# Plain down blocks and the u3 sums reach the residual by accumulating transfers, in a two-layer GLA and stick-breaking decoder trunk

## The chip, the core and the metric

The kernel runs on one core of a Trainium2 chip. The metric is the device time of one execution, in microseconds. The core's engines work side by side: TensorE multiplies matrices (PE in the profile), VectorE (DVE), ScalarE (ACT), GpSimd (POOL) and SyncE (SP), whose work here is to issue transfers. Sixteen DMA engines carry the transfers of all queues. Each engine runs its own instructions in order and waits on semaphores for what other engines or transfers have to deliver.

## The reference, cut to what is computed

One input `x` of 512 tokens by 1024 features in float32 passes two layers. Each is an FFN with half a step, a mixer, and a second FFN with half a step; a final RMSNorm ends it.

```python
def swiglu(h, w_gate, w_up, w_down):
    return (jax.nn.silu(h @ w_gate) * (h @ w_up)) @ w_down

for i in range(DEPTH):                       # DEPTH = 2
    x = x + 0.5 * swiglu(rmsnorm(x, ffn1_norm[i]), ffn1_w_gate[i], ffn1_w_up[i], ffn1_w_down[i])
    h = rmsnorm(x, mix_norm[i])
    y = gla_mixer(...) if i % N_MIXERS == 0 else sb_mixer(...)
    x = x + y
    x = x + 0.5 * swiglu(rmsnorm(x, ffn2_norm[i]), ffn2_w_gate[i], ffn2_w_up[i], ffn2_w_down[i])
return rmsnorm(x, final_norm)
```

So there are four FFNs: the first, the second after the gated linear attention, the third, and the last after the stick-breaking attention. The hidden width of an FFN is 2816, that is 11 chunks of 256 columns.

## The kernel before, in words

**The residual.** It stays on the core, transposed: eight tiles `xs[0]` to `xs[7]` of 128 features by 512 tokens in float32. Every down product of an FFN adds half of its result to one of these tiles.

**Products in parts.** TensorE multiplies each float32 product as three: every weight and every activation is split into a high and a low part, and high x high, low x high and high x low are added in one PSUM bank (`mm3`, line 80). The split of a weight is a cast on ScalarE (`wh`, L138) and a subtraction on VectorE (`wl`, L139). Weights arrive in blocks of 1 MB for gate and up (tile `raw`, two buffers) and 512 KB for down (`rawd`), issued on SyncE's queue at L105.

**The FFN.** `FFN.GROUPS` cuts the 11 chunks into six groups: chunks 0-1, 2-3, 4-5, 6-7, 8 and 9-10. A group's gate and up products give hidden tiles; its down products follow while the next group's gate and up run. Three kinds of product occur.

- *Seven products* for gate and up (`seven`): a Strassen-like scheme computes a 2x2 block product in seven instead of eight. VectorE first forms sums of weight blocks, `sums_12` and `sums_34` (L704, L705, L710, L711), from the raw block into a tile `s`; these sums are then split like weights. In PSUM the banks `ps_w`, `ps_q` and `ps_z` are built up over several products. ScalarE copies `ps_w` into `ps_z` (L746), so that TensorE can go on in both; later it copies an intermediate sum into the tile `u3` (L764), and VectorE adds it (L765).
- *Seven downs* (`seven_down`) for groups 1 and 3, in the same scheme. Their result is added to the residual a quarter at a time by `add` on VectorE (L396). One intermediate sum, `u3`, belongs to two quarters: ScalarE copies it from PSUM (L435), VectorE adds the copy to the right half of a tile of the upper residual half, and the bank is used on for other quarters.
- *Plain downs* (`down`) for groups 0, 2, 4 and 5. Each call is a part: `n` parts in a group of `n` hidden blocks, with `8 / n` residual tiles in each. For the tiles that `homes` names, ScalarE writes half of the PSUM bank into a tile `d` (L340), and a transfer that accumulates, on GpSimd's queue, adds it to the residual tile (L341, 256 KB). For the others VectorE adds half of the bank to the residual itself (L345).

`HOMES` (L624) lists per group which tiles go by transfer, by the tag of the place that holds `d`: `("d",)` for groups 0 and 2, `("d", "ss", "sq")` for group 4; the places are single. `ss` and `sq` also hold the sums of squares and the factor `R` of the norm, and the t34 parts of the seven downs. The gate and up sevens' `u3` is tagged `c` in the pool `tp`, with one buffer, and the seven downs' `u3` shares it.

**The order of the work.** Each engine's order is set by a planner of the framework, which places the instructions by its own costs; TensorE's order follows a queue of entries (`feed.q`), one per weight block, and many pieces are pinned behind the last matmul. A place is written again only when its last reader, a transfer too, is done.

**The end.** In the last FFN the down products of the last group are computed with tokens on partitions (`back_tok`). Before them `to_tokens` transposes the eight residual tiles on TensorE into `ps_T` (L1570), and ScalarE copies them back (L1575); the final norm follows on the tokens.

The list of groups and the part of the code that hands the homes on:

```python
GROUPS = ((0, 2), (2, 4), (4, 6), (6, 8), (8, 9), (9, 11))
DOWN_SEVEN = (1, 3)
HOMES = {0: ("d",), 2: ("d",), 4: ("d", "ss", "sq")}
...
homes = self.HOMES.get(group, ())
downs = [
    (wd, c0 * 256, n, self.hs[group], part, nxt if end else None, 0, homes) for part in range(n)
]
```

Of the kernel before, what the change touches and what calls it, by code (L numbers as in the profile page):

```python
# [10 lines left out]
F32 = mybir.dt.float32  # L11
# [3 lines left out]
AF = mybir.ActivationFunctionType  # L15
ALU = mybir.AluOpType
PSUM = bass.MemoryType.PSUM

P = 128
T = 512  # L20
# [10 lines left out]
def turns(t):  # L31

    return t.rearrange("p (two n) -> p n two", two=2)


def flat(ps):

    return ps.rearrange("p (n two) -> p two n", two=2)


def pair(t):

    return t.rearrange("p (two n) -> p two n", two=2)
# [3 lines left out]
def decoder(ctx: ExitStack, tc: tile.TileContext, a: dict, out: bass.AP):  # L47
    nc = tc.nc
# [6 lines left out]
    sp = ctx.enter_context(tc.tile_pool(name="sp", bufs=1))  # L55
# [5 lines left out]
    def psum(name, tag=None):  # L61
        if tag is None:
            tag = order[turn_[0] % 8]
            turn_[0] += 1
        return pp.tile([P, T], F32, tag=tag, bufs=banks[tag], name=name)
# [11 lines left out]
    xs = [xp.tile([P, T], F32, name=f"x{k}") for k in range(KD)]  # L77
# [4 lines left out]
    def mm3(ps, wh, wl, mh, ml, first, last):  # L82
        mm(ps, wh, turns(mh), first, False)
        mm(ps, wl, turns(mh), False, False)
        mm(ps, wh, turns(ml), False, last)
# [223 lines left out]

                feed.q.append(Entry([u], body))  # L310

    def down(w, r0, nf, hs, part, nxt, late=0, homes=()):


        nd = KD // nf
        src = w[r0 : r0 + nf * P, part * nd * P : (part + 1) * nd * P]
        ch = Chunk(src.rearrange("(f p) c -> p f c", p=P), nf, nd * P)
        ch.few = True

        def body(W):  # L320
            (wh, wl), = W
            acc = []

            def prod(m, fs):
                if m == len(acc):
                    acc.append(psum("ps_d"))
                s = slice(m * P, (m + 1) * P)
                for f in fs:
                    mm3(acc[m], wh[:, f, s], wl[:, f, s], hs[f][0], hs[f][1], f == 0, f == nf - 1)

            if late:
                for m in range(nd):
                    prod(m, range(nf - late))
            for m in range(nd):
                prod(m, range(nf - late if late else 0, nf))
                ps = acc[m]
                k = part * nd + m
                if m < len(homes):
                    d = sp.tile([P, T], F32, tag=homes[m], name="d")
                    nc.scalar.activation(pair(d), flat(ps), AF.Copy, scale=0.5)  # L340
                    nc.gpsimd.dma_start(xs[k], d, accum_op=ALU.add)  # L341
                    yield
                    continue
                x = pair(xs[k])
                nc.vector.scalar_tensor_tensor(  # L345
                    out=x, in0=flat(ps), scalar=0.5, in1=x, op0=ALU.mult, op1=ALU.add
                )
                if nxt is not None:
                    nxt(k)
                yield  # L350

        feed.q.append(Entry([(ch, lambda t: t, nf, nd * P)], body))

    def seven_down(pool, w, r0, hs, part):

        H = T // 2
        lower, upper = (
            Chunk(w[r0 : r0 + 4 * P, c : c + 256].rearrange("(f p) c -> p f c", p=P), 4, 256)  # L360
            for c in (part * 256, 512 + part * 256)
        )
        lower.few = upper.few = True
        v = {}

        def halves():

            lo, up = (c.load().rearrange("p (c two) d -> p two c d", two=2) for c in (lower, upper))
            return lo[:, 0], lo[:, 1], up[:, 0], up[:, 1]

        def sums_12(_):
            a11, _, a21, a22 = halves()
            s = v["s12"] = pool().tile([P, 4, 256], F32, tag="s", bufs=4, name="s12")
            nc.vector.tensor_tensor(out=s[:, 0:2], in0=a21, in1=a22, op=ALU.add)
            nc.vector.tensor_tensor(out=s[:, 2:4], in0=s[:, 0:2], in1=a11, op=ALU.subtract)
            return s

        def sums_34(_):
            a11, a12, a21, _ = halves()
            s = pool().tile([P, 4, 256], F32, tag="s", bufs=4, name="s34")  # L380
            nc.vector.tensor_tensor(out=s[:, 0:2], in0=a11, in1=a21, op=ALU.subtract)
            nc.vector.tensor_tensor(out=s[:, 2:4], in0=a12, in1=v["s12"][:, 2:4], op=ALU.subtract)
            return s

        def prod(ps, w, k0, m, b, first):
            for c in range(2):
                bh, bl = (turns(t) for t in hs[c][b])
                wh, wl = (t[:, k0 + c, m * P : (m + 1) * P] for t in w)
                for n, (l_, r_) in enumerate(((wh, bh), (wl, bh), (wh, bl))):
                    st["pe"] = nc.tensor.matmul(  # L390
                        ps, l_, r_, start=first and c + n == 0, stop=c == 1 and n == 2, skip_group_check=True
                    ).ins

        def add(m, up, col, ps):
            x = pair(xs[part * 2 + m + 4 * up][:, col * H : col * H + H])
            nc.vector.scalar_tensor_tensor(out=x, in0=ps, scalar=0.5, in1=x, op0=ALU.mult, op1=ALU.add)  # L396

        def body_1(W):
            a11, s, v["a2"] = W
            ws, zs, qs = [], [], []  # L400
            for m in range(2):
                ws.append(psum("ps_w")[:, 0:H])
                prod(ws[m], a11, 0, m, "b11", True)
            for m in range(2):


                zs.append(psum("ps_z")[:, 0:H])
                nc.scalar.copy(zs[m], ws[m])
            yield

            ps = psum("ps_q")
            for m in range(2):
                qs.append(ps[:, m * H : (m + 1) * H])
                prod(qs[m], s, 0, m, "t1", m == 0)
            for m in range(2):
                add(m, 1, 1, flat(qs[m]))
            yield
            for m in range(2):
                prod(ws[m], s, 2, m, "t2", False)
                add(m, 0, 1, flat(ws[m]))  # L420
            yield
            for m in range(2):
                prod(zs[m], v["a2"], 0, m, "b21", False)
                add(m, 0, 0, flat(zs[m]))
            v["w"], v["q"] = ws, qs
            yield

        def body_2(W):
            (s,) = W
            ws, qs = v["w"], v["q"]  # L430

            u3 = pool().tile([P, 2, H], F32, tag="c", bufs=1, name="u3")
            for m in range(2):
                prod(ws[m], s, 0, m, "t3", False)
                nc.scalar.copy(pair(u3[:, m]), flat(ws[m]))  # L435
                add(m, 1, 1, pair(u3[:, m]))
            yield
            for m in range(2):
                prod(qs[m], s, 2, m, "b22", False)
            for m in range(2):  # L440
                add(m, 0, 1, flat(qs[m]))
            yield
            for m in range(2):
                prod(ws[m], v["a2"], 2, m, "t4", False)
                add(m, 1, 0, flat(ws[m]))
            yield

        units = [(lower, lambda t: halves()[0], 2, 256), (lower, sums_12, 4, 256), (lower, lambda t: halves()[1::2], 4, 256)]
        feed.q.append(Entry(units, body_1))
        feed.q.append(Entry([(lower, sums_34, 4, 256)], body_2))  # L450

    def back_tok(w, r0, nf, hs, done):
# [160 lines left out]
    class FFN:  # L613
# [7 lines left out]
        NORMED, SEVEN, AHEAD = 6, 2, 2  # L621
        DOWN_SEVEN = (1, 3)
        SEVEN_UP = (2, 3, 4, 5, 6, 7, 8, 9, 10)
        HOMES = {0: ("d",), 2: ("d",), 4: ("d", "ss", "sq")}  # L624

        def __init__(self, wg, wu, wd, gi, nxt, first=False, last=False):
            self.gi, self.normed = gi, False
# [4 lines left out]
            base, downs, late = len(feed.q), [], []  # L632
            self.sums_by = 10**6
            for group, (c0, c1) in enumerate(self.GROUPS):
                slots, put = 2 * (c1 - c0), 0
                if group == 1:

                    for put in range(self.AHEAD):
                        down(*downs[put][:6], late=put == 0, homes=homes)
                    put = self.AHEAD  # L640
                for i in range(slots):
                    c, f = c0 + i // 2, i % 2
                    if f == 0:
                        g, u = Chunk(cols(wg, c * 256, 256), KD, 256), Chunk(cols(wu, c * 256, 256), KD, 256)
                    d = self.defer if i == 0 and c == 0 else None
# [30 lines left out]
                for x in downs[put:]:  # L676
                    down(*x)
                n = 2 * (c1 - c0)
                end = group + 1 == len(self.GROUPS)
                homes = self.HOMES.get(group, ())  # L680
                downs = [
                    (wd, c0 * 256, n, self.hs[group], part, nxt if end else None, 0, homes) for part in range(n)
                ]
                if group in self.DOWN_SEVEN:
                    downs = []
# [1228 lines left out]
```

## Time and profile before

| | |
|---|---|
| median of 3 runs | 1779.24 us (1779.19 to 1779.93) |
| profiled execution | 1779.44 us |
| its span in the trace | 1777.5 us |
| TensorE busy | 1756.3 us, 12714 instructions |
| VectorE busy | 1508.6 us, 2471 |
| ScalarE busy | 1081.6 us, 1886 |
| GpSimd busy | 58.4 us, 80 |
| moved by DMA | 193.93 MB |

The profile is of one execution: its span runs from the first to the last instruction recorded, and its own time has 1.9 us around that span. Busy times are sums over an engine's instructions, with waits left out. In a row of a group stand the line, the engine, the operation, the tile written and the tiles read, the shapes and the count, then the busy sum and the mean in ns of one, then the idle time ahead of them and what ended most of it. In the chain of waits each row is a start, a duration and the work that the end of the kernel depended on. In a timeline row the brackets hold the engine's idle time just before it and who ended it.

### The profile page before, as it was taken

How to read it: one execution, taken by the hardware profiler on the slowest of the kernel's cores; microseconds unless marked ns; L12 is line 12 of the kernel's file. 1: busy time of each engine (PE TensorE's matmuls, PEld its weight loads, DVE VectorE, ACT ScalarE, POOL GpSimd, SP SyncE). 2: the span in 40 equal slices, each digit the busy share in tenths (PEclk: the TensorE clock that was granted, in tenths of full speed). 3: DMA queues.
4: the chain of work that ended last, by engine and by line, in shares of the span. 5: the costliest groups of instructions: out<-in, count | busy, mean ns of one | idle time of the engine just before them, and what ended most of it. 6: DMA issues, size and time to landing. Idle time of an engine off the chain costs nothing.

```text
span 1777.5 us, 31388 instructions
## 1 busy us (share of the span) xinstructions
PE 1756.3 (99%) x12714; PEld 1630.4 (92%) x12714; DVE 1508.6 (85%) x2471; ACT 1081.6 (61%) x1886; POOL 58.4 (3%) x80
## 2 busy tenths in 40 slices
PE   9999999999999999999999999999999999999998
PEld 8999999889888899999889999999888888999997
DVE  8999797786888989888798988967898679997985
ACT  7556556554655556555565555555889745665655
POOL 0000000200000000000000000010000000000000
PEclk9999999999999999999999999999999999999999
DMA  5543435422123433344424344342212134434342
GB/s 168 153 120 118 125 103 148 112 72 72 49 95 95 130 108 119 119 119 126 141 85 130 103 124 135 110 120 83 84 49 78 66 95 131 131 108 129 114 131 65
DMA packets 186820, 193.93 MB, mean 109 GB/s; under 512 B 4978, under 2 KB 171172, under 8 KB 186676
## 3 DMA queue, kind: packets, MB, share of 16 engines
q1 hardware_dynamic: 177760, 175.91, 31.7%
q0 software_dynamic: 8672, 15.74, 4.9%
q8 instruction: 99, 1.62, 0.4%
q14 instruction: 45, 0.37, 0.1%
q10 hardware_dynamic: 244, 0.29, 0.0%
HBM read 175.17 MB, written 2.10 MB: 100 GB/s over the span
## 4 chain that ended last, share of the span: by engine, by line
PE 67%; DVE 22%; ACT 5%; DMA 3%; issue 3%; POOL 0%; DVEq 0%; SPq 0%; ACTq 0%; POOLq 0%
PE ps_w L719 16%; PE ps_d L80 11%; PE ps_q L719 8%; PE ps_f L80 7%; DVE wl L139 5%; PE ps_t L80 4%; PE ps_z L719 4%; PE ps_w L390 4%; PE ps_b L80 3%; PE ps_q L390 2%; ACT wh L138 2%; DMA raw<-in_ffn_w_gate_dram 1%; DVE ts L826 1%; PE ps_z L1402 1%; DVE nl L817 1%
## 5 line engine op out<-in xcount | busy, mean ns | idle before, releaser
L139 DVE TENSOR_TENSOR wl<-raw,wh 128x1024 fp32r<-128x1024 f32 x241 | 255.0, 1059 | 59.8 <-ACT wh L138 59.1
L138 ACT CAST wh<-raw 128x1024 fp32r<-128x1024 f32 x241 | 221.7, 921 | 77.1 <-PE ps_f L80 22.6
L139 DVE TENSOR_TENSOR wl<-s,wh 128x1024 fp32r<-128x1024 f32 x176 | 214.3, 1218 | 47.2 <-ACT wh L138 47.2
L719 PE MATMUL ps_w<-th,wh 128*128 128x256 f32 x864 | 239.4, 277 | 4.2 <-ACT ps_z L746 4.1
L719 PE MATMUL ps_w<-th,wl 128*128 128x256 f32 x864 | 237.6, 275 | 0.0
L719 PE MATMUL ps_w<-tl,wh 128*128 128x256 f32 x864 | 237.6, 275 | 0.0
L138 ACT CAST wh<-s 128x1024 fp32r<-128x1024 f32 x176 | 184.1, 1046 | 69.1 <-DVE s L705 19.3
L719 PEld LDWEIGHTS ps_w<-th,wh 128*128 128x128 f32 x864 | 165.8, 192 | 7.6 <-ACT ps_z L746 7.6
L80 PE MATMUL ps_f<-xh,wh 128*128 128x512 f32 x432 | 166.4, 386 | 0.0
L719 PEld LDWEIGHTS ps_w<-tl,wh 128*128 128x128 f32 x864 | 165.9, 192 | 0.0
L719 PEld LDWEIGHTS ps_w<-th,wl 128*128 128x128 f32 x864 | 165.8, 192 | 0.0
L80 PE MATMUL ps_f<-xh,wl 128*128 128x512 f32 x432 | 164.2, 380 | 0.5 <-DVE wl L139 0.5
L80 PE MATMUL ps_f<-xl,wh 128*128 128x512 f32 x432 | 163.9, 379 | 0.0
L80 PE MATMUL ps_d<-hl,wh 128*128 128x512 f32 x416 | 158.0, 380 | 1.7 <-DVE hl L817 1.7
L80 PE MATMUL ps_d<-hh,wh 128*128 128x512 f32 x416 | 158.0, 380 | 0.5 <-ACT hh L816 0.5
L80 PE MATMUL ps_d<-hh,wl 128*128 128x512 f32 x416 | 157.7, 379 | 0.0
L139 DVE TENSOR_TENSOR wl<-rawd,wh 128x1024 fp32r<-128x1024 f32 (+1 forms) x100 | 96.0, 963 | 16.0 <-ACT wh L138 15.8
L138 ACT CAST wh<-rawd 128x1024 fp32r<-128x1024 f32 (+1 forms) x100 | 82.8, 845 | 39.3 <-PE ps_d L80 25.6
L341 POOL DMA_DIRECT2D x<-d x56 | 48.6, 879 | 1531.1 <-ACT d L340 829.9
L80 PEld LDWEIGHTS ps_f<-xl,wh 128*128 128x128 f32 x432 | 81.6, 189 | 11.5
L80 PEld LDWEIGHTS ps_f<-xh,wl 128*128 128x128 f32 x432 | 81.7, 189 | 11.3 <-DVE wl L139 0.9
L80 PEld LDWEIGHTS ps_f<-xh,wh 128*128 128x128 f32 x432 | 81.7, 189 | 10.8
(355 smaller groups left out, 5324.9 us busy)
## 6 DMA issues: line engine op xcount, KB each, us to landing
raw<-in_ffn_w_gate_dram SPq DMA_DIRECT2D x43, 1024.0 KB, 5.5
raw<-in_ffn_w_up_dram SPq DMA_DIRECT2D x43, 1024.0 KB, 5.4
rawd<-in_ffn_w_down_dram SPq DMA_DIRECT2D x84, 512.0 KB, 3.7
x<-d POOLq DMA_DIRECT2D x56, 256.0 KB, 4.6
raw<-in_gla_w_in_dram SPq DMA_DIRECT2D x12, 1024.0 KB, 5.3
raw<-in_sb_w_in_dram SPq DMA_DIRECT2D x16, 512.0 KB, 3.8
raw<-in_gla_w_out_dram SPq DMA_DIRECT2D x4, 1024.0 KB, 5.0
raw<-in_sb_w_in_dram SPq DMA_DIRECT2D x4, 1024.0 KB, 5.2
```

What stands on the lines that cost most here:

```text
L80: st["pe"] = nc.tensor.matmul(ps, l, r, start=first, stop=last).ins
L138: st["cut"] = nc.scalar.copy(h[:, k], part).ins
L139: nc.vector.tensor_tensor(out=l[:, k], in0=part, in1=h[:, k].bitcast(F32), op=ALU.subtract)
L341: nc.gpsimd.dma_start(xs[k], d, accum_op=ALU.add)
L390: st["pe"] = nc.tensor.matmul(ps, l_, r_, start=first and c + n == 0, stop=c == 1 and n == 2, skip_group_check=True).ins
L719: st["pe"] = nc.tensor.matmul(o, l_, r_, start=first and j + n == 0, stop=j == 3 and n == 2, skip_group_check=True).ins
L817: nc.vector.tensor_tensor(out=l, in0=t, in1=h.bitcast(F32), op=ALU.subtract)
L826: nc.vector.tensor_tensor(out=o, in0=p, in1=q, op=ALU.subtract)
L1402: nc.tensor.matmul(o_, l_, r_, start=first, stop=last, skip_group_check=True)
```

## The change

Two things change. First, `HOMES` names places for each part of a group. All plain downs of group 0 and group 2 now go by transfer, two of each part: those of group 0's first, third and fourth part and of all parts of group 2 through `d` and `c`, those of group 0's second part through `ss` and `sq`. In group 4 (one chunk, two parts of four tiles) the first part goes by transfer through `d`, `c`, `ss` and `sq`; of the second part two tiles go through `d` and `c`, and in the last FFN none. A place named `c` is the one in `tp` that the `u3` tiles use. The plain downs of group 5 stay as they are.

Second, the `u3` of the seven downs is scaled by 0.5 as ScalarE copies it, and a transfer of 128 KB on GpSimd's queue adds it to the upper residual half, in place of VectorE's `add`.

```diff
@@ down(w, r0, nf, hs, part, nxt, homes, pool, late=0)
                 if m < len(homes):
-                    d = sp.tile([P, T], F32, tag=homes[m], name="d")
+                    own = homes[m] == "c"
+                    d = (pool() if own else sp).tile([P, T], F32, tag=homes[m], bufs=1, name="d")
                     nc.scalar.activation(pair(d), flat(ps), AF.Copy, scale=0.5)
                     nc.gpsimd.dma_start(xs[k], d, accum_op=ALU.add)
@@ seven_down, body_2
             for m in range(2):
                 prod(ws[m], s, 0, m, "t3", False)
-                nc.scalar.copy(pair(u3[:, m]), flat(ws[m]))
-                add(m, 1, 1, pair(u3[:, m]))
+                nc.scalar.activation(pair(u3[:, m]), flat(ws[m]), AF.Copy, scale=0.5)
+                nc.gpsimd.dma_start(xs[part * 2 + m + 4][:, H:T], u3[:, m], accum_op=ALU.add)
             yield
@@ FFN
-        HOMES = {0: ("d",), 2: ("d",), 4: ("d", "ss", "sq")}
+        HOMES = {
+            0: (("d", "c"), ("ss", "sq"), ("d", "c"), ("d", "c")),
+            2: (("d", "c"),) * 4,
+            4: (("d", "c", "ss", "sq"), ("d", "c")),
+        }
...
-                        down(*downs[put][:6], late=put == 0, homes=homes)
+                        down(*downs[put], late=put == 0)
...
-                homes = self.HOMES.get(group, ())
+                homes = self.HOMES.get(group, ((),) * n)
+                if last and group == 4:
+                    homes = (homes[0], ())
                 downs = [
-                    (wd, c0 * 256, n, self.hs[group], part, nxt if end else None, 0, homes) for part in range(n)
+                    (wd, c0 * 256, n, self.hs[group], part, nxt if end else None, homes[part], lambda: self.tp)
+                    for part in range(n)
                 ]
```

In the changed kernel's own numbering the lines move: L340 and L341 become L341 and L342, L345 becomes L346, L396 becomes L397, L435 becomes L436 with the new transfer at L437, L704 to L711 become L712 to L719, L746 becomes L754, L764 and L765 become L772 and L773, and L1570 becomes L1578.

More of the change, by code (lines that the diff above doesn't have):

```diff
@@ L310, in back, with down @@
                 feed.q.append(Entry([u], body))
-    def down(w, r0, nf, hs, part, nxt, late=0, homes=()):
+    def down(w, r0, nf, hs, part, nxt, homes, pool, late=0):
         nd = KD // nf
```

## The prediction

> **What bounds the kernel now.** I read the page first: engine shares, DMA queues, then the chain that ended last.
>
> ```profile
> span 1777.5 us, 31388 instructions
> PE 1756.3 (99%) x12714; PEld 1630.4 (92%) x12714; DVE 1508.6 (85%) x2471; ACT 1081.6 (61%) x1886; POOL 58.4 (3%) x80
> q1 hardware_dynamic: 177760, 175.91, 31.7%
> q0 software_dynamic: 8672, 15.74, 4.9%
> PE 67%; DVE 22%; ACT 5%; DMA 3%; issue 3%; POOL 0%; DVEq 0%; SPq 0%; ACTq 0%; POOLq 0%
> ```
>
> TensorE is the bound, and the time can fall only where it stands still. So the next view is who TensorE waited for.
>
> ```profile
> PE ps_w L719 <- ACT ps_z L746: 4.1, 10, 1.2
> PE ps_T L1570 <- DMA x<-d: 1.6, 2, 0.8
> ```
>
> VectorE holds 22% of the chain, but freeing it pays only where one of these stalls starts with it. The longest is the ps_z copy. The chain of waits in order of time shows its first case, ahead of 77.4 us, and another ahead of 947 us has the same form:
>
> ```profile
> 63.61 0.61 DVE s L711
> 64.29 7.07 DMA raw<-in_ffn_w_gate_dram
> 71.38 0.04 DVE s L704
> 73.21 0.60 DVE s L705
> 73.81 0.35 DVE o L765
> 77.06 0.28 ACT ps_z L746
> 77.38 1.60 PE ps_w L719 x12
> 78.99 1.34 PE ps_z L719 x12
> ...
> 931.83 7.61 DMA raw<-in_ffn_w_gate_dram
> ```
>
> A gate load is issued when VectorE has read the last block. VectorE then waits for its landing, forms sums, reaches the addition L765, and ScalarE behind it is late with ps_z. What delays that load or puts work ahead of L765 goes straight to TensorE.
>
> **What it moves, by price.** These are the rows of the groups, the transfers' durations, and the gate loads:
>
> ```profile
> L345 DVE SCALAR_TENSOR_TENSOR x<-ps_d,x 128x512 f32<-128x512 f32 x64 | 43.6, 685 | 30.6 <-PE ps_d L80 30.6
> L396 DVE SCALAR_TENSOR_TENSOR x<-u,x 128x256 f32<-128x256 f32 x32 | 12.0, 415 | 0.0
> L340 ACT ACTIVATE d<-ps_d 128x512 f32<-128x512 f32 x56 | 33.1, 595 | 26.7 <-PE ps_d L80 22.5 <-DMA x<-d 3.8
> L435 ACT COPY u<-ps_w 128x256 f32<-128x256 f32 x32 | 12.0, 375 | 21.4 <-PE ps_w L390 21.4
> L341 POOL DMA_DIRECT2D x<-d x56: 851/862/1214, 59.5 to 1744.5; - x56
> DMA to landing us min/median/max: 3.3/4.6/8.4
> raw<-in_ffn_w_gate_dram SPq DMA_DIRECT2D x43, 1024.0 KB, 5.5
> ```
>
> Plain downs by transfer go from 14 to 22 in each of the first three FFNs and to 20 in the last: 56 to 86. VectorE loses 30 x 0.685 + 32 x 0.415 = 33.8 us. ScalarE gains 30 x 0.595 = 17.9 us; the 32 u3 copies stay copies (0.375 us), now with a factor. POOL issues 62 more transfers, 62 x 0.862 = 53 us on a queue that is 3% busy; nothing but transfers waits behind them there. A 256 KB transfer costs about 0.049 x 1777.5 / 56 = 1.55 us of all 16 DMA engines (an upper estimate, since q0 carries a few others), a 128 KB one half of it. The 62 add 30 x 1.55 + 32 x 0.78 = 71 us, 4% of the span: no bound as a mean, but it comes in bursts. The orders of TensorE and SP are unchanged; POOL's only gains entries, with the last FFN's gain load kept in its place among them.
>
> **The end of the kernel (a gain).** The last FFN's second part of the fifth group goes back to VectorE, so TensorE no longer waits for landings before its transposes:
>
> ```profile
> 1744.40 0.69 DVE L345 SCALAR_TENSOR_TENSOR x<-ps_d,x 128x512 f32<-128x512 f32 x1 [1.55 <-PE ps_d L80]
> ...
> 1744.51 4.29 DMA x<-d
> 1748.84 1.09 PE ps_T L1570 x8
> 1749.94 15.56 PE ps_bt L80 x72
> ```
>
> VectorE finishes the last block 0.7 us after TensorE (1745.1), before TensorE has turned the first four tiles. Both waits of the list go (1.6 us); with the restarts it may be 2.1. If VectorE is 0.6 us behind, its tile is still ahead of its transpose. I take -1.8 (0 to -2.1).
>
> **VectorE's freed time in the FFNs: nearly nothing.** In the changed program's order the gaps that the 62 instructions leave are filled: later sums are moved up. An example is the queue before the stall at 1670 us, between these two:
>
> ```profile
> 1658.82 0.68 DVE L345 SCALAR_TENSOR_TENSOR x<-ps_d,x 128x512 f32<-128x512 f32 x1
> 1666.51 0.42 DVE L765 TENSOR_TENSOR o<-u,o 128x256 f32<-128x256 f32 x1
> ```
>
> The L345 is gone, and a sum that stood behind L765 now stands ahead of it: as many instructions as before. The same holds for the stalls of this form in the other FFNs. Where TensorE waits for the additions L396 themselves I take -0.3 (0 to -0.7).
>
> **The first sevens of two FFNs (a loss).** In the first FFN the new order puts two further sums (0.60 us each) between the gate load's landing and L765, +1.2; one L345 less ahead of the load lets it start 0.6 earlier. In the third FFN a sum that needs the load is moved ahead of a low part that does not:
>
> ```profile
> 937.11 1.21 DVE L139 TENSOR_TENSOR wl<-s,wh 128x1024 fp32r<-128x1024 f32 x1
> 939.46 0.69 DVE L704 TENSOR_TENSOR s<-raw 128x512 f32<-128x512 f32 x1 [1.14 <-DMA raw<-in_ffn_w_gate_dram]
> ```
>
> So the 1.2 us low part, done at 937 before the landing, now comes after it and ahead of L765: +1.1, and the gate load is issued no earlier. Beside both loads run two more 256 KB transfers: contention adds 0 (the median load takes 5.5) to 2.1 each (this one took 7.6 with two transfers near it); I take 0.6 each, since these loads already show most of it. Together 1.2 - 0.6 + 1.1 + 1.2 = +2.9 (+1.7 to +5.9).
>
> The Trainium skill, page DMA: Bandwidth & Descriptors, section Queues, rings and completion order, says that each DMA engine takes turns between queue rows packet by packet. By that rule an overlapping 256 KB transfer would cost a load its whole time, an estimate of 1.55 us each here; the two long gate loads agree with it.
>
> **The u3 transfers (a loss).** Two 128 KB transfers leave just when a gate load is issued. From the third FFN and the first:
>
> ```profile
> 1009.35 0.37 ACT L435 COPY u<-ps_w 128x256 f32<-128x256 f32 x1 [0.25 <-PE ps_w L390]
> 1010.28 6.42 DMA raw<-in_ffn_w_gate_dram
> ...
> 140.31 0.37 SPq L105 DMA_DIRECT2D raw<-in_ffn_w_gate_dram  x1
> 146.27 0.68 DVE L704 TENSOR_TENSOR s<-raw 128x512 f32<-128x512 f32 x1
> ```
>
> In the third FFN VectorE is already waiting for this load; half of the 1.55 us gives +0.8. In the others the sum starts some 0.5 us after a median landing, and VectorE comes 0.8 us earlier without its two additions, so only 0.2 each is left: +1.4 together (0 to +1.5 + 3 x 0.9 = 4.2).
>
> **The new waits on ScalarE.** Tile "c" also holds the u3 of the gate and up sevens, so ScalarE's copy L764 now waits for the landing of the down before it:
>
> ```profile
> 1614.26 0.69 DVE L345 SCALAR_TENSOR_TENSOR x<-ps_d,x 128x512 f32<-128x512 f32 x1 [2.67 <-PE ps_d L80]
> 1620.96 0.37 ACT L764 COPY u<-ps_w 128x256 f32<-128x256 f32 x1 [1.36 <-PE ps_w L719]
> ```
>
> The copy into "c" will start where this L345 did and take 0.6; 6.1 us later u3 is wanted. The issue 0.1 us later and the median landing of 4.6 leave 1.4. The casts of later weights stand behind L764 on ScalarE, and TensorE may reuse the bank one product later (1.34 - 0.37 = 0.97 more). Only landings above 7.0 reach TensorE; against the median 4.6 few of the 56 can be. There are 6 such places in each FFN; I charge 0.5 (0 to 24 x (8.4 + 0.1 - 6.1 - 0.97) = 34, far off, since only the closest triples of transfers came near 8.4, and these come in pairs 2.6 us apart). The fifth group's waits on "c", "ss" and "sq" are one per FFN and lie in this range.
>
> **Sum.** -1.8 - 0.3 + 2.9 + 1.4 + 0.5 = +2.7. The profiled execution took 1779.44 us (span 1777.5 and 1.9 around it), 0.2 above the median 1779.24 of the three runs shown: 1779.4 + 2.7 = 1782.1. What a measurement of this kernel can tell from no change is 0.2%, 3.6 us: 1775.7 to 1782.8.
>
> **Rivals.**
> - *Loads slowed in full (slower).* Place: the gate loads of the two first sevens and those beside the u3 pairs. For it: 7.07 and 7.61 against a median of 5.5. Against it: a median gate load leaves VectorE some slack. Price: 2.1 in place of 0.6 at two places (+3.0) and 4.2 in place of 1.4: 1782.1 + 5.8 = 1787.9. It decides once an added pair costs a load more than about 1 us.
> - *"c" holds ScalarE (slower).* Pairs land 1.6 us later for their overlap and each issue waits for one VectorE instruction of 1.2 us: 4.6 + 2.8 = 7.4 against 7.0, 24 x 0.4 = +10: 1792. It decides at a landing of 7.0. Against it: the issues lie at 851 to 862 ns in the median with VectorE 85% busy. The Trainium skill, page GPSIMD Engine Reference, section 1. Specifications, has GpSimd contend for its SBUF interfaces with VectorE instructions that have two SBUF inputs, which speaks for such late issues; the trace's even issue times do not agree.
> - *VectorE's relief reaches the stalls (faster).* 34 us less work lets gate loads start earlier and halves the ps_z waits: -2.1 and their restarts -1.5, with the end's -1.8: 1774. Against it stands the order above.
> - *All hidden but the end.* Sums moved up cost nothing, loads keep their slack: 1779.4 - 1.8 = 1777.6.
>
> **How the numbers follow.** The forecast, 1782.1 with its own range 1779.5 to 1785: 0.42, of it 0.27 within 0.2% and 0.15 above. Loads in full 0.24, "c" 0.06, both slower. Relief 0.16, of it 0.14 faster and 0.02 within. Hidden 0.12, within. Faster 0.14, same 0.41, slower 0.45. From 1775 to 1789 some 2 in 10 are left out: most of the relief, "c", and the upper part of the slow loads.
>
> **What would show it.** Right: no ps_T wait on a transfer; ps_z waits larger ahead of 77 and 947 us, the others of L746 as before; gate loads beside the transfers at 6 to 8 us; DVE near 1475 and ACT near 1100 us busy; L764 waiting little for x<-d. Wrong: ps_z waits that fall; many long waits of ACT u for x<-d; gate loads that keep 5.5 us.

## The result and the profile after

| kernel | median of the runs | lowest to highest | ratio to before, 95% interval |
|---|---|---|---|
| before, beside it | 1779.24 us (7 runs) | 1778.80 to 1780.51 | |
| changed | 1785.59 us (7 runs) | 1781.79 to 1788.64 | 1.0032 [1.0021, 1.0044] |
| changed, once more (`a_again`) | 1783.12 us (11) | 1779.36 to 1785.75 | 1.0018 [1.0009, 1.0027] |
| changed, a third time (`a_third`) | 1783.39 us (8) | 1781.24 to 1786.61 | 1.0020 [1.0010, 1.0030] |

The changed kernel is slower by 0.2 to 0.3% (each ratio is to the kernel before that ran beside it). The forecast was 1782.1, its range 1775 to 1789. The profiled execution took 1781.79 us, 2.35 more than the profiled one of before, but it was the fastest of its seven: the median lies 3.8 us above it. Both numbers need an explanation, and they have different ones.

Three lines of the page of the changed kernel (the last is the queue that carries GpSimd's transfers), and then, from its list of waits, the work that TensorE waited for (total us, times, longest us):

```profile
span 1779.7 us, 31517 instructions
PE 1756.6 (99%) x12714; PEld 1631.4 (92%) x12714; DVE 1482.1 (83%) x2409; ACT 1095.8 (62%) x1916; POOL 112.0 (6%) x142
q0 software_dynamic: 17600, 27.80, 9.3%
...
PE ps_w L727 <- ACT ps_z L754: 8.8, 15, 2.1
PE ps_d L80 <- DVE hl L825: 1.7, 2, 0.8
```

VectorE lost 26.5 us of work, and TensorE, whose own work is the same, did not get one of them: the execution is longer. The list of waits has changed at two places: the transposes' wait for a landing is gone, and the wait for ps_z has grown from 4.1 to 8.8 us, from 10 times to 15.

The end first. The chain of waits of the changed kernel between 1744 and 1754 us has no transfer in it any more:

```profile
1743.88 4.75 PE ps_d L80 x22
1748.63 3.49 PE ps_T L1578 x32
1752.12 1.94 PE ps_bt L80 x9
```

The 32 transposes run without a break, in 3.49 us; before, they waited 0.8 us twice. This is the gain.

The loss is seen at the longest wait. The chain of waits between 1008 and 1031 us, in the third FFN:

```profile
1012.98 7.42 DMA raw<-in_ffn_w_gate_dram
1020.40 0.02 issue
1020.42 0.69 DVE s L712
...
1024.65 0.60 DVE s L376
1025.26 0.35 DVE o L773
1025.60 0.02 issue
1025.63 0.42 ACT o L737
1026.05 0.93 ACT wh L138
1026.98 0.59 ACT o L737 x2
1027.57 0.93 ACT wh L138
1028.50 0.28 ACT ps_z L754
1028.78 0.04 issue
1028.83 1.60 PE ps_w L727 x12
```

The gate load beside the two u3 transfers takes 7.42 us, 6.42 before. Between its landing and the addition L773 stands one sum more, L376, which was L375 behind the addition L765 in the kernel before. VectorE's timeline of the kernel before at this place:

```profile
1020.88 0.42 DVE L765 TENSOR_TENSOR o<-u,o 128x256 f32<-128x256 f32 x1
1021.21 0.68 DVE L375 TENSOR_TENSOR s<-s,rawd 128x512 f32<-128x512 f32 x1
```

Then follow the same ScalarE steps, and TensorE waits 2.1 us where it waited 0.5. Counted from the start of one matmul to the start of the next, five such places grew by 3.4 us in all and the two first sevens (76 and 948 us) by 1.1; one restart at 1607 us came 0.3 sooner, which leaves 4.2.

The transfer durations of the changed kernel (the DMA issues: count, KB each, median us to landing) show what the u3 pairs cost by themselves:

```profile
raw<-in_ffn_w_gate_dram SPq DMA_DIRECT2D x43, 1024.0 KB, 5.6
x<-d POOLq DMA_DIRECT2D x86, 256.0 KB, 4.2
x<-u POOLq DMA_DIRECT2D x32, 128.0 KB, 3.0
```

### The profile page after: what moved, and what is told of

Read it like the earlier page. It is cut to its first block, busy times and chain, and to the rows that moved or that the text cites. A ratio compares the mean times of both kernels' runs of the same rounds, so it can differ in the third digit from the quotient of the medians.

```text
span 1779.7 us, 31517 instructions
## 1 busy us (share of the span) xinstructions
PE 1756.6 (99%) x12714; PEld 1631.4 (92%) x12714; DVE 1482.1 (83%) x2409; ACT 1095.8 (62%) x1916; POOL 112.0 (6%) x142
## 4 chain that ended last, share of the span: by engine, by line
PE 64%; DVE 23%; ACT 6%; issue 3%; DMA 3%; DVEq 0%; ACTq 0%; SPq 0%
PE ps_w L727 15%; PE ps_d L80 13%; PE ps_q L727 7%; PE ps_f L80 7%; DVE wl L139 6%; PE ps_t L80 4%; PE ps_z L727 4%; PE ps_w L391 3%; PE ps_b L80 3%; DMA raw<-in_ffn_w_gate_dram 3%; ACT wh L138 2%; PE ps_q L391 1%; DVE ts L834 1%; PE ps_z L1410 1%; DVE xn L818 1%
## 5 line engine op out<-in xcount | busy, mean ns | idle before, releaser
L727 PEld LDWEIGHTS ps_w<-th,wh 128*128 128x128 f32 x864 | 165.8, 192 | 11.9 <-ACT ps_z L754 11.7
L342 POOL DMA_DIRECT2D x<-d x86 | 74.2, 878 | 1064.0 <-ACT d L341 570.6
L341 ACT ACTIVATE d<-ps_d 128x512 f32<-128x512 f32 x86 | 51.3, 596 | 71.2 <-PE ps_d L80 71.0
```

What stands on the lines that cost most here:

```text
L727: st["pe"] = nc.tensor.matmul(o, l_, r_, start=first and j + n == 0, stop=j == 3 and n == 2, skip_group_check=True).ins
```

## The experiments

### Which part: the end, the u3, the plain downs

Three kernels carry one part each; all ran beside the unaltered changed kernel.

The end alone, `b_end`, on the kernel before:

```diff
-                    (wd, c0 * 256, n, self.hs[group], part, nxt if end else None, 0, homes) for part in range(n)
+                    (wd, c0 * 256, n, self.hs[group], part, nxt if end else None, 0, () if last and group == 4 and part else homes) for part in range(n)
```

> The kernel before, with only the last FFN's second part of the fifth group put back on VectorE (its three transfers gone). Theory: the two waits of the transposes at the end go (1.6 us, 2.0 with their restarts), nothing else moves: -2.0, 1777.3. Rival: VectorE finishes the last block too late and takes their place: 0 to -0.5.

Measured: 1777.46 us against 1779.37, ratio 0.9986 [0.9978, 0.9995], -1.9 us. As expected; the chain of its trace from 1738 to 1752 us has the transposes without a break:

```profile
1738.84 5.18 PE ps_d L80 x24
1744.02 3.49 PE ps_T L1570 x32
1747.51 4.54 PE ps_bt L80 x21
```

The u3 alone, `c_u3`, on the kernel before:

```diff
-                nc.scalar.copy(pair(u3[:, m]), flat(ws[m]))
-                add(m, 1, 1, pair(u3[:, m]))
+                nc.scalar.activation(pair(u3[:, m]), flat(ws[m]), AF.Copy, scale=0.5)
+                nc.gpsimd.dma_start(xs[part * 2 + m + 4][:, H:T], u3[:, m], accum_op=ALU.add)
```

> The kernel before, with only the u3 of the seven downs by transfer (32 transfers of 128 KB, 32 additions fewer on VectorE). Theory 'order': the sum L375 is planned ahead of the addition L765 in five places of four FFNs, 0.6 us each, and in the third FFN VectorE also waits for a slower gate load, about 1: +4.0, 1783.2, with ps_z waits of about 0.5 at 155, 270, 700 and 1587 us and 2 at 1026. Theory 'contention': only what the gate loads lose counts, +1.4 (my forecast): 1780.6. If these transfers also carry the lower clock, the median of its runs is 3 to 4 above its profile at clock 1.000.

Measured: 1782.76 us, ratio 1.0017 [1.0008, 1.0026], +3.4. The waits for ps_z are there at the five places. So the u3 part alone costs about what the whole change costs.

The plain downs and the end, without the u3, `d_homes`, is the changed kernel with those two lines turned back.

> The changed kernel with the u3 of the seven downs as before (copy and addition on VectorE): the plain downs by transfer and the end alone. Theory: first sevens +1.1 (the ps_z waits ahead of 77 and 947 us), end -2.0, and no stalls of 0.5 us at 155, 270, 700, 1587 us: -0.9, 1778.4. Rival 'c holds ScalarE': waits of L764's copy for x<-d reach TensorE: above 1782. If the plain downs' transfers carry the lower clock, its runs spread over 5 us or more and lie 3 to 4 above its profile.

Measured: 1779.11 us, ratio 1.0003 [0.9993, 1.0012]. The two longest waits of ps_z in its trace are at the first sevens, as expected; the profile is 0.7 above the sum, and two of its eleven runs stand at 1783.5 and 1783.9 with a granted clock of 0.998 and 0.997. Nothing in it speaks for a ScalarE held by "c". Its -0.3 and the +3.4 of the u3 alone add up to 3.1 of the 3.75 that the changed kernel lost beside them.

The changed kernel itself, once more:

> The changed kernel once more, unaltered. Its first profile (1781.8 us, granted clock 1.000) accounts for the sum of the stalls, but the median of its runs is 1785.6, and the runs above 1783 show a mean granted clock of 0.998 to 0.996. Theory 'clock': the excess over 1781.8 is time at a lower granted clock; the TensorE stalls stay those of the first profile within 1 us, and the missing 0.2% of clock (some 3.6 us) sits in a few stretches. Theory 'landings': the excess is in the ps_z stalls, whose loads land later in some executions; their sum is then 8.8 us plus the excess. Both expect 1782 to 1788.

Measured: 1783.12 us, and a profile at 1779.36, again the fastest of its runs; the sum of its stalls is no more than that of the first profile. What makes the other runs longer is not in this trace; the experiments on the clock, below, bear on it.

### Order or contention at the five places

`c_u3` does two things at once: it takes 32 additions out of VectorE's queue, whose gaps the planner then fills with sums from further down, and it adds 32 transfers. Two kernels do one each. `c_none` leaves the transfers out of `c_u3`; VectorE's order stays exactly that of `c_u3`.

```diff
                nc.scalar.activation(pair(u3[:, m]), flat(ws[m]), AF.Copy, scale=0.5)
-                nc.gpsimd.dma_start(xs[part * 2 + m + 4][:, H:T], u3[:, m], accum_op=ALU.add)
```

> The u3 alone of the kernel before, with neither the addition nor the transfer: the u3 of the seven downs is copied and added nowhere, so one of the sums of the upper residual half is left out. VectorE's order is that of c_u3, instruction for instruction; only the 32 transfers are gone. Theory 'order': the ps_z waits of about 0.5 us at 154, 269, 699 and 1584 us stay, and some 0.4 of the one at 1024: 1781.4. Theory 'contention': they go with the transfers: 1779.4.

`c_both` keeps the transfers and gives VectorE an instruction in the place of each addition (in 12 of the 16 parts one of the two stands one instruction away from it):

```diff
                nc.gpsimd.dma_start(xs[part * 2 + m + 4][:, H:T], u3[:, m], accum_op=ALU.add)
+                junk = sp.tile([P, H], mybir.dt.bfloat16, tag="junk", bufs=1, name="junk")
+                nc.vector.scalar_tensor_tensor(
+                    out=pair(junk), in0=pair(u3[:, m]), scalar=0.5, in1=pair(u3[:, m]), op0=ALU.mult, op1=ALU.add
+                )
```

> The u3 by transfer, with VectorE doing an instruction of the addition's shape beside it, whose result nobody reads: VectorE's order is that of the kernel before, with the 32 transfers added. Theory 'order': the waits of 0.5 us are not there, only the 1024 us place shows what its gate load loses, 0.6 to 1: 1780.2. Theory 'contention': as c_u3, 1782.8.

Measured: `c_none` 1780.05 us, ratio 1.0005 [0.9996, 1.0014]; `c_both` 1780.50, ratio 1.0007 [0.9998, 1.0016]; `c_u3` was 1.0017. Neither theory holds alone: each half costs little. The medians by themselves do not show that the halves cost more together, since the intervals overlap; the waits do: the four shorter ones (154, 269, 699 and 1584 us) are 0.24 to 0.44 us in `c_u3` and at most 0.1 in the other two. The traces of the changed kernel have them too (11 of the 12), and none without the transfers has. VectorE's timeline at the first place shows how. First `c_u3`, then `c_none`, then `c_both`:

```profile
144.88 0.68 DVE L139 TENSOR_TENSOR wl<-raw,wh 128x512 fp32r<-128x512 f32 x1
145.98 0.69 DVE L704 TENSOR_TENSOR s<-raw 128x512 f32<-128x512 f32 x1 [0.42 <-DMA raw<-in_ffn_w_gate_dram]
...
150.13 0.68 DVE L375 TENSOR_TENSOR s<-s,rawd 128x512 f32<-128x512 f32 x1
150.74 0.42 DVE L765 TENSOR_TENSOR o<-u,o 128x256 f32<-128x256 f32 x1
```

```profile
145.27 0.68 DVE L139 TENSOR_TENSOR wl<-raw,wh 128x512 fp32r<-128x512 f32 x1
145.88 0.68 DVE L703 TENSOR_TENSOR s<-raw 128x512 f32<-128x512 f32 x1
```

```profile
146.29 0.69 DVE L139 TENSOR_TENSOR wl<-raw,wh 128x512 fp32r<-128x512 f32 x1
146.89 0.68 DVE L708 TENSOR_TENSOR s<-raw 128x512 f32<-128x512 f32 x1
```

With the order of before and the transfers (`c_both`), VectorE is busy until the slower load has landed. With the new order and no transfers (`c_none`), it comes earlier, and the load is there. With both (`c_u3`), it comes earlier and the load comes later: it idles 0.42 us there, and since L375 stands ahead of L765 all the same, the addition comes about that much later; TensorE's matmul at 154.40 then waits 0.44 us for ps_z. The slack of one place was used up twice.

The place at 1024 us had no such slack: it waits 1.4 us in `c_none`, 1.5 in `c_both` and 1.5 in `c_u3`, with loads of 6.65, 7.48 and 6.85 us.

### What makes the median longer than the sum: the clock

Every trace ends with a fall of the clock, after TensorE's last work. A trace with a fall in the midst came by chance, in the profile of `c_none`, at the first seven of the third FFN. The windows of its trace (window, length, then per engine the busy time and its instructions, PE first; the last three numbers are the granted clock, the DMA share and GB/s):

```profile
941.77:945.18 3.41, 3.41 (x33) 3.41 (x33) 3.19 (x6) 0.52 (x2) 0.00 (x0) 1.00 0.00 0
945.18:948.59 3.41, 1.54 (x14) 1.35 (x13) 2.25 (x2) 3.41 (x7) 0.00 (x0) 1.00 0.88 276
948.59:952.00 3.41, 3.41 (x18) 3.41 (x18) 1.26 (x3) 1.35 (x3) 0.00 (x0) 0.50 0.14 39
```

TensorE's own timeline around it:

```profile
945.72 0.28 PE L718 MATMUL ps_q<-tl,wh 128*128 128x256 f32 x1
947.86 0.38 PE L718 MATMUL ps_w<-th,wh 128*128 128x256 f32 x1 [1.87 <-ACT ps_z L745]
...
948.66 0.42 PE L718 MATMUL ps_w<-th,wh 128*128 128x256 f32 x1
```

TensorE waits 1.87 us for ps_z. From 948.59 on the granted clock is 0.50 for exactly 3.41 us, each matmul takes 0.42 instead of 0.28, and 18 are recorded where a full window holds 33: 1.6 us of work are lost by this count, 1.7 by the half clock, nearly as much as the wait itself.

`ladder` asks for the rule. It repeats the ps_z copy at six places of the kernel before:

```diff
-                nc.scalar.copy(z, w)
+                n = st["nz"] = st.get("nz", -1) + 1
+                for _ in range({5: 7, 13: 10, 23: 13, 31: 16, 59: 19, 67: 23}.get(n, 1)):
+                    nc.scalar.copy(z, w)
```

> The kernel before, with the ps_z copy repeated at six places where TensorE already waits 0.3 us for it: 6, 9, 12, 15, 18 and 22 more copies at 125, 240, 670, 785, 1554 and 1670 us, some 0.3 us each, so waits of about 2, 3, 4, 5, 6 and 7 us. Theory 'clock gate': above a length somewhere between 2 and 4 us the trace shows the granted clock at 0.5 right behind the wait, for some 3 to 7 us, each costing half of that: 1779.4 + 25 of waits + 4 times 2 to 3 = 1812 to 1816. Theory 'stalls only': the clock stays at 1.00 behind all of them: 1804.

Measured: 1826.04 us, +46.7, more than both theories gave, because a copy took about 0.4 us instead of 0.3 and the six waits became 3.1 to 9.4 us. The sum of the ps_z waits is 39.2 us in its trace, 4.1 before, so 35.1 are waiting, and 11.6 are left for the time at half clock (46.7 is of medians; the traced execution was 1.4 shorter). There are five falls. The one shown below costs half of its busy 2.30 + 3.41 us, 2.9; the five together, counted in the same way, cost 11.7. Five of the six waits made the clock fall, the shortest did not. The windows around the shortest and the second:

```profile
123.85:127.26 3.41, 1.73 (x16) 1.54 (x14) 3.38 (x5) 3.35 (x10) 0.00 (x0) 1.00 0.54 187
127.26:130.68 3.42, 2.01 (x18) 2.01 (x19) 2.26 (x4) 1.66 (x7) 0.00 (x0) 1.00 0.00 0
130.68:134.09 3.41, 3.41 (x33) 3.41 (x32) 2.28 (x5) 1.42 (x4) 0.00 (x0) 1.00 0.23 63
...
243.32:246.73 3.41, 0.21 (x2) 0.02 (x1) 3.41 (x5) 3.25 (x11) 0.00 (x0) 1.00 0.08 23
246.73:250.15 3.42, 2.30 (x11) 2.30 (x11) 0.80 (x2) 1.01 (x3) 0.00 (x0) 0.50 0.02 5
250.15:253.56 3.41, 3.41 (x18) 3.41 (x17) 0.88 (x2) 1.41 (x3) 0.00 (x0) 0.50 0.01 2
```

All five falls of this trace lie on one grid of 3.41 us, whatever the waits, and each ends only behind a window in which TensorE was busy throughout: 2.30 us of work at half clock did not end it. The wait of 3.1 us at 125 us, cut by a line of that grid into two windows of 1.73 and 2.01 us busy, passes, while the wait of 1.87 in `c_none`, which lies within one window and leaves it 1.54 busy, does not. So it is the busy share of a window that decides, with a threshold between 1.54 and 1.73 of 3.41 us as far as these rows go. The other traces agree: of the windows at full clock in all thirteen, each one with 1.54 us of work or less was followed by a half window, and none with more; the nearest above is one of the changed kernel at 1771.29, with 1.65. So a wait of about 2 us falls or passes by its place on the grid. The profile of the changed kernel passed in this way, at its longest wait:

```profile
1023.77:1027.19 3.42, 2.99 (x27) 2.80 (x26) 2.34 (x5) 1.56 (x3) 0.00 (x0) 1.00 0.31 79
1027.19:1030.60 3.41, 1.77 (x15) 1.77 (x16) 3.37 (x4) 2.53 (x7) 0.00 (x0) 1.00 0.65 228
```

The Trainium skill, page TensorE: Matmul & The Clock Gate, section Part 1: The HAM clock gate (the "warmup" mystery), has the clock fall to a half after an idle window of some 3.4 us on a free-running grid. The grid, the length and the half are as in these traces; if an idle window is one without any work, the rule is stricter than what these traces show, since 1.54 us of work did not help.

Then the one place in the changed kernel: `e_one` turns the u3 back for the first part of the third FFN's second group, and leaves the other 15 parts.

> The changed kernel with the u3 of one part as before: the first part of the third FFN's second group, beside the gate load of 1013 us; the other 15 parts by transfer. Its trace loses the longest wait, 2.3 us at 1024, down to 0.65. Theory 'clock gate': that wait is long enough in most executions to drop the granted clock to a half for some microseconds; without it the runs come back to a clock of 0.999 and the median falls by more than the stall, from 1783.1 to 1779 to 1780. Theory 'stalls only': it falls by the 1.6 us of the stall alone, to 1781.5, and runs at 0.998 stay as frequent (7 of 11).

Measured: 1780.38 us, ratio 1.0011 [1.0002, 1.0019], against 1783.12 of the changed kernel in the earlier comparison (1.0018). The longest ps_z wait in its trace is 1.3 us. The fall of 2.7 is more than the 1.6 of the stall, and 3 of 11 runs are at 0.998 instead of 7 of 11; that points to the clock, but the two intervals overlap, and the changed kernel itself has only 3 such runs of 8 in `a_third`, below.

The changed kernel a third time, for a trace with the fall in it:

> The changed kernel once more, to find an execution whose trace holds a fall of the clock. Theory 'clock gate': if the mean clock is 0.998 or less, the trace has a window of 3.41 us at 0.5 behind a wait of 2 us or more at 1026 or 948 us, lying in the window just before it; if it is 0.999 or 1.000, no window of 3.41 us is idle for more than 2 us.

Measured: 1783.39 us. The profiled execution was again among the shortest, 1781.66 at 0.999, so this was not caught; no window of the grid in the stretch of an FFN is idle for more than 1.5 us. Over the 26 executions of the changed kernel, 16 have a clock of 0.998 or less, with a median of 1784.9, and 10 a higher one, with a median of 1781.7; of the executions of the kernel before, none of the 60 that ran beside `a_again` and `c_none` has 0.998 or less, but 6 of the 27 beside `a_third` have. One window at half clock is 1.7 us or 0.001 of the mean clock. Between the two sets of the changed kernel the mean clock differs by 0.0016, which is 2.9 us of 1782, and the mean time by 2.9 us: the lower clock is enough for the excess of these runs. That the falls of the changed kernel sit at 948 and 1026 us is inferred from the waits; no trace of it shows one.

### The first sevens

`f_g24` is `d_homes` with the first group as before; `g_g0dve` is `b_end` with the first group wholly on VectorE.

```diff
-            0: (("d", "c"), ("ss", "sq"), ("d", "c"), ("d", "c")),
+            0: (("d",),) * 4,
```

```diff
-        HOMES = {0: ("d",), 2: ("d",), 4: ("d", "ss", "sq")}
+        HOMES = {2: ("d",), 4: ("d", "ss", "sq")}
```

> The changed kernel with u3 as before and the first group as before (one plain down of each part by transfer): only the third and fifth groups by transfer, and the end. Theory 'first sevens': the ps_z waits ahead of 77 and 947 us go back to 1.2 and 1.3 (from 1.6 and 1.9 in d_homes), nothing else stalls: -2.0 of the end alone, 1777.4, as b_end. Rival: the third group's transfers cost something of their own by their gate loads: 1779.

> b_end with the first group's plain downs all on VectorE, so that no transfer runs beside the gate loads of 64 and 932 us. Theory 'contention': those loads fall from 7.1 and 7.6 to the median 5.5 and the two longest ps_z waits shrink by up to 1 each: 1775.5 to 1777. Theory 'order': VectorE's added instructions (0.6 us each) ahead of the same loads take it back or more: 1777.5 to 1779.

Measured, beside a before of 1779.91 us: `f_g24` 1777.05, ratio 0.9983 [0.9974, 0.9992]; `g_g0dve` 1780.16, ratio 1.0002 [0.9993, 1.0011]. So the third and fifth groups by transfer cost nothing that these runs can tell (the interval holds the -2.0 of the end), which leaves the first group for what `d_homes` lost; the two ran on different chips, and their intervals are just apart. The trace of `f_g24` does not confirm the expected size of single waits: its longest, at 947 us, is 1.9, not 1.3. That wait moves between 1.0 and 1.8 from trace to trace of the changed kernel (1.7, 1.0 and 1.8). In `g_g0dve` VectorE's extra work took back all of the 1.9 of the end, but not where 'order' put it. The wait at 76 us fell from 1.0 to 0.2, as 'contention' has it, the one ahead of 950 us stayed at 1.2, and TensorE's restarts, counted start to start, grew by 2.5 us in the second FFN and 0.8 in the last, in many small waits, for ps_z above all. So neither theory describes this kernel.

`b_end` and `f_g24` both beat the kernel before, by 0.14% and 0.17%, by the same end; they ran on different chips, and which is the better is open.

## Why the prediction was right and wrong

Against its own profile the sum came out: +2.7 forecast, +2.35 measured. That it came so near is in part luck: three terms missed by 1.8, 1.7 and 0.5 us and cancelled, and the two other profiled executions of the changed kernel took 1779.36 and 1781.66, no more than the median before beside the one and 1.75 above it beside the other. Its terms:

- *The end, -1.8.* Right: -2.0 in the trace, -1.9 as the median of `b_end`.
- *L396, -0.3.* Nothing: the additions that TensorE waited for are late as before (at three places before, at four after, by 0.15 to 0.3 us each).
- *First sevens, +2.9 (1.7 to 5.9).* Over-sized, and below its range: +1.1 in the trace (0.65 at 76 us, 0.4 at 948), 0.4 and 1.1 in the other two. The step that failed is the contention charged in full on top of the order: the gate loads took 7.12 and 6.78 us, 7.07 and 7.61 before. The two 256 KB transfers that were added did not slow them.
- *The u3 transfers, +1.4 (0 to 4.2).* Under-sized: +3.1 in the trace. The mechanism was right (VectorE comes 0.8 earlier and a later landing catches it), but I gave 0.2 to each of three places, and 0.8 to the third FFN. Four shorter waits grew by 0.45 each in the mean, the one at 1026 by 1.6, about half of it by the moved sum L376, which this term left out: `c_none` shows 1.4 us at that place without any transfer.
- *New waits on ScalarE, +0.5.* Nothing in time. In the profile all 72 waits of the copy into u3 end with TensorE's product, none with a landing; in each of the other two traces one of them, near 1730 us, waits for a landing (1.2 and 1.5 us), and TensorE does not. From the waits of ScalarE in the changed kernel:

```profile
ACT u L772 <- PE ps_w L727: 85.7, 72, 1.4
```

- *Issue on GpSimd at nothing.* Right; 860 ns in the median with 86 issues of 256 KB, as with 56:

```profile
L342 POOL DMA_DIRECT2D x<-d x86: 848/860/1214, 59.9 to 1725.6; - x86
L437 POOL DMA_DIRECT2D x<-u x32: 860/991/1132, 140.5 to 1717.5; - x32
```

- *VectorE's work, -33.8.* Over-sized. The durations that are gone add up to that (20.5 and 13.3 us), but the busy time fell by 26.5, and by 27.2 and 26.2 in the other two traces. Instructions that follow each other at once overlap in the record (one of 0.68 us starts at 145.27 above, the next at 145.88), and busy time counts an overlap once.

So the terms of the trace are -2.0 + 1.1 + 3.1 = +2.2.

What the sum left out altogether is the clock: its durations came from profiled executions in which no fall took place, and the median of the runs is 1785.6, 3.8 above. The forecast called the time within 0.2% likely at 0.41 and slower at 0.45; it was slower by 0.32%, and in the other two comparisons, by 0.18 and 0.20%, on the border.

Of the rivals, "loads slowed in full" at 1787.9 is refuted as a mechanism though its time is near: the loads beside the u3 pairs took 5.8 to 5.9 us in place of 5.3 to 5.5 at 141, 687 and 1573 us, 7.5 in place of 6.7 at 257 and 7.4 in place of 6.4 at 1013. Over all eight such loads, two transfers of 128 KB cost 0.2 to 1.0, not their own 1.55. The rule of the Trainium skill, page DMA: Bandwidth & Descriptors, section Queues, rings and completion order, that DMA engines take turns packet by packet, gives an upper bound here, as the prediction read it. "c holds ScalarE" did not occur, but for one copy in each of two traces. "VectorE's relief" did not reach a stall: 26.5 us less work, and no wait on it of more than 0.3 us became shorter. "Hidden but the end" fits the third and fifth groups alone.

## What to carry to other kernels

A relief of an engine that is not the bound pays only where a named stall begins with it; the planner fills the gap with later work, and the stall keeps its place or gets worse. Slack at one place may cover either an earlier arrival or a later landing, but not both: when an edit changes two things that lean on the same slack, cost them together. A stall of TensorE of around 2 us is worth more than its length, since it can be followed by a window at half clock; look at the longest stall first, and compare the profiled execution with the other runs before a sum of its waits is trusted.

## What the runs showed of the hardware

The granted clock falls to 0.50 for whole windows of 3.41 us, when TensorE was busy for 1.54 us or less of the window before; with 1.65 us or more it did not fall. The kernel does not set the grid of these windows: its first line lies 0.6 us after the first instruction in the trace of the kernel before and 3.2 in that of the changed one. A busy window at half clock costs 1.7 us. So a wait of 1.9 us can cost twice its length in one execution and nothing more in the next, and the spread of the changed kernel's runs (7 us in the first comparison, where that of the kernel before is 1.7) is a sign of it.

An accumulating transfer within the chip of 128 KB landed in 3.0 us in the median of 32, but in 6.4 to 7.6 us as the second of a pair with a gate load beside it, and a pair slowed that load by 0.2 to 1.0 us: the small transfer suffers more than the large one; its issue took 0.86 us on GpSimd for the first and 1.12 to 1.13 for the second of a pair.
